# A recurrent scan's transfers on SyncE in a written order, weights fetched three tiles ahead, and a transposition queued late

## The chip, the cores and the metric

The kernel runs on one core of one Trainium2 chip. The metric is the device time of one execution in microseconds. The core has TensorE (PE in the profile; its weight loads are PEld), VectorE (DVE), ScalarE (ACT), GpSimd (POOL) and SyncE (SP). Each takes its instructions in order; DMAs are started here by SyncE or ScalarE, and the start stands in that engine's order (SPq, ACTq).

## The reference, cut to what matters

A two-layer decoder trunk over 272 tokens (16 learned ones and 256 given), model width 2048, all float32. The first layer mixes tokens with an RWKV-7 recurrence, the second with stick-breaking attention; each is followed by a SwiGLU block. The change touches the recurrence alone: for each of 32 heads of width 64

```python
def step(state, inp):
    r_t, d_t, k_t, v_t, kk_t, a_t = inp
    sa = jnp.einsum('bhvk,bhk->bhv', state, -kk_t)
    state = (state * d_t[:, :, None, :]
             + sa[..., None] * (kk_t * a_t)[:, :, None, :]
             + v_t[..., None] * k_t[:, :, None, :])
    return state, jnp.einsum('bhvk,bhk->bhv', state, r_t)
...
_, y = lax.scan(step, s0, tuple(seq_first(t) for t in (rh, dh, kh, vh, kk, ah)))
y = seq_first(y)
...
y = ((y - mean) * lax.rsqrt(var + GN_EPS)).reshape(b, l, d) * gn_w + gn_b
bonus = (jnp.sum(rh * kh * r_k, axis=-1, keepdims=True) * vh).reshape(b, l, d)
out = ((y + bonus).astype(h.dtype) * g) @ w_o
```

with `r`, `k`, `v` from the products of the shifted tokens with `w_r`, `w_k`, `w_v`, and the decay, the rate `a` and the gate `g` from small two-step (low-rank) products.

## The kernel before, in words

Tokens lie along the free axis (272 columns), features along the 128 partitions. A product of float32 weights is made in three matmuls: `split` (or the two lines L167 and L168 of `parts`) turns a weight tile `raw` into a rounded part `whi` (ScalarE) and the rest `wlo` (VectorE), and `mm3k` (L186 to L188) multiplies `whi` by both parts of the activations and `wlo` by the first.

The recurrence is worked in four chunks of 64 tokens and one of 16, for a pair of heads at a time: 16 pairs, class `Pair`. `scan` runs a software pipeline over periods n = -3 to 15. In period n four pairs are at work: C (pair n+3) makes its decay and rate in `lora`; B (n+2) makes its scores, has the 16x16 diagonal blocks of its triangular system solved on GpSimd in `solve`, and lays out its operands; M (n+1) joins the solved blocks into 64x64 inverses in `left(16)`, `right(16)`, `left(32)`, `right(32)`, then `apply` and `trans`; A (n) passes the state through the chunks in `states` and `step`, and then `norm` and `gate` make its output `o` (L1286). Between these calls `f` takes a few steps of `stream`, which multiplies the tokens by the big weights `w_v`, `w_r` and at the end `w_o`: 32 steps of three matmuls in a full period, so four tiles `raw` of 512 KB; `raw` has three buffers, `whi` and `wlo` six each.

The order of TensorE in the scan is that of the program, written out by hand (`manual_schedule`). All other engines, and SyncE's transfers with them, are ordered when the kernel is built by a planner, which places what it expects to be ready, by its own times.

The path of a pair's solve, with the lines in the profile: scores `G` (VectorE, L1071) go by DMA to a scratch tile `s1` in DRAM (L1076, L1078: four issues), the diagonal blocks come back as `As` (L1080); GpSimd solves them into `Ts` (L1109 to L1116); `Ts` goes by DMA to `s2` (L1118), and 64x64 tiles `Tt` come back (L1121, two issues). All eight are issued from ScalarE (`self.dq = nc.scalar`). `left` transposes `Tt` into `Tn` on VectorE (L1170) and multiplies `Tt` (`yb`, L1174); `right` multiplies with `Tn` (`zb`, L1193) and adds to `Tt` (L1194). `apply` ends with `Ah` (VectorE, L1209), which `trans` multiplies (`rm`, L1221). `norm` sums squares over each head on TensorE (`vb`, L951), takes a logarithm and an exponential on ScalarE (L1271, L1272, each with a load of its function table), and goes on with five VectorE instructions (L1273 to L1277); `gate` adds `o`.

The small weights of a pair (`w2` in `split_w`, L933: 128 KB each; the name in the trace is `lora`) and the norms `rn` (L961) come by SyncE, as the big weights do (L156).

## The time and the profile before

| | us |
|---|---|
| median of 3 runs | 2808.99 (2807.55 to 2813.99) |
| the profiled execution's own time | 2810.86 |
| its span, first to last instruction | 2809.0 |
| TensorE busy in the span | 2688.8 |
| VectorE, ScalarE, GpSimd busy | 1797.5, 1489.9, 178.8 |
| mean granted TensorE clock | 0.981 of full speed |

The profile is of one execution. "Busy" is the union of an engine's instructions. A line of the view of waits reads: who waited, for whom, how long in total, how often, the longest. A line of the timeline reads: start, duration, engine and line, operation, what it writes from what, how many, and in brackets the idle time of the engine before it with what ended it. The scan lies where GpSimd solves: its L1116 starts first at 209.4 and last at 708.1 us.

### The profile page before, as it was taken

Reading aid. Unit: us, or ns where it says so; the run is one execution under the profiler, and the core shown is the slowest. Engines: PE = TensorE matmul, PEld = TensorE weight load, DVE = VectorE, ACT = ScalarE, POOL = GpSimd, SP = SyncE. Lnnn points to the kernel's source line nnn. Section 1 sums busy time; section 2 is a strip of 40 time slices with the busy share of each in tenths; the row PEclk is TensorE's granted clock in tenths of the full one; section 3 lists DMA queues with packets and bytes.
Section 4 is the critical chain, followed back from the end, with each engine's and each line's share of the span. In section 5 each row is a group of like instructions: output and inputs, shape, how many; then the busy total and the mean of one; then the engine's idle time right before and its main releaser. Section 6 shows DMA issues by size and latency. Waiting matters only on the chain.

```text
span 2809.0 us, 54126 instructions
## 1 busy us (share of the span) xinstructions
PE 2688.8 (96%) x20942; PEld 2484.5 (88%) x20942; DVE 1797.5 (64%) x3586; ACT 1489.9 (53%) x3005; POOL 178.8 (6%) x539
## 2 busy tenths in 40 slices
PE   7987888888899999999999999999999999999999
PEld 5787777777799999999999999988888888888888
DVE  6665666666466555555555776577776666666666
ACT  6664555555455444444444665477655455455554
POOL 0004333333000000000000000000000000000000
PEclk9999999999899999999999999999999999999999
DMA  5443333332455555555565555533456565665655
GB/s 178 128 127 101 96 92 86 86 85 77 137 170 179 166 185 176 165 186 175 166 186 176 164 178 166 173 128 120 156 186 188 184 193 178 200 188 179 196 185 175
DMA packets 185330, 439.50 MB, mean 156 GB/s; under 512 B 58448, under 2 KB 88688, under 8 KB 185072
## 3 DMA queue, kind: packets, MB, share of 16 engines
q1 hardware_dynamic: 140240, 426.67, 48.0%
q10 hardware_dynamic: 44832, 9.38, 1.7%
q8 instruction: 164, 2.69, 0.4%
q14 instruction: 94, 0.77, 0.1%
HBM read 430.24 MB, written 5.74 MB: 155 GB/s over the span
## 4 chain that ended last, share of the span: by engine, by line
PE 83%; POOL 6%; DMA 4%; ACT 2%; DVE 2%; issue 2%; ACTq 1%; POOLq 0%; DVEq 0%; SPq 0%
PE mm L192 22%; PE mm L186 14%; PE mm L188 14%; PE mm L187 14%; PE mm L191 11%; POOL Ts L1116 3%; POOL Tm L1114 3%; PE lr L540 1%; DMA As<-s 1%; DMA s<-Ts 1%; DMA raw<-w_k 1%; ACT whi L167 1%; PE cb L1255 1%; DMA s<-G 1%; PE hms L791 1%
## 5 line engine op out<-in xcount | busy, mean ns | idle before, releaser
L168 DVE TENSOR_TENSOR wlo<-raw,whi 128x512 fp32r<-128x512 f32 (+1 forms) x1588 | 1076.6, 682 | 676.5 <-ACT whi L167 655.5
L167 ACT CAST whi<-raw 128x512 fp32r<-128x512 f32 (+1 forms) x1588 | 962.3, 611 | 946.0 <-PE mm L187 558.5
L186 PE MATMUL mm<-hl,whi 128*128 128x272 f32 x3344 | 982.2, 294 | 6.8 <-ACT whi L167 5.1
L188 PE MATMUL mm<-hl,wlo 128*128 128x272 f32 x3344 | 973.7, 291 | 4.0 <-DVE wlo L168 4.0
L187 PE MATMUL mm<-hl,whi 128*128 128x272 f32 x3344 | 971.0, 290 | 0.0
L192 PE MATMUL mm<-hl,whi 128*128 128x512 f32 x2624 | 920.0, 395 | 0.0
L191 PE MATMUL mm<-hl,wlo 128*128 128x256 f32 x2624 | 740.8, 283 | 0.0
L186 PEld LDWEIGHTS mm<-hl,whi 128*128 128x128 f32 x3344 | 636.6, 190 | 19.0 <-issue 8.6
L187 PEld LDWEIGHTS mm<-hl,whi 128*128 128x128 f32 x3344 | 643.1, 192 | 0.6
L188 PEld LDWEIGHTS mm<-hl,wlo 128*128 128x128 f32 x3344 | 637.0, 191 | 6.3 <-DVE wlo L168 4.7
L192 PEld LDWEIGHTS mm<-hl,whi 128*128 128x128 f32 x2624 | 492.5, 188 | 113.0
L191 PEld LDWEIGHTS mm<-hl,wlo 128*128 128x128 f32 x2624 | 494.2, 188 | 0.6
L208 DVE TENSOR_TENSOR h<-h,mm 128x256 f32<-128x256 f32 (+1 forms) x224 | 94.0, 421 | 6.6 <-PE mm L192 6.0
L186 PE MATMUL mm<-hi,whi 128*128 128x272 f32 x256 | 80.8, 316 | 0.0
L201 ACT COPY c<-mm 128x256 f32<-128x256 f32 x104 | 38.8, 373 | 78.8 <-PE mm L192 78.7
L1116 POOL TENSOR_TENSOR Ts<-Ts,Tm 40x14 f32<-40x14 f32 (+6 forms) x224 | 77.7, 347 | 17.5
L1114 POOL TENSOR_TENSOR Tm<-Ts,As 40x14 f32<-40x14 f32 (+6 forms) x224 | 75.5, 337 | 17.5
L187 PE MATMUL mm<-lo,whi 128*128 128x272 f32 x256 | 74.9, 293 | 0.0
L188 PE MATMUL mm<-hi,wlo 128*128 128x272 f32 x256 | 74.6, 291 | 0.0
L1221 PE MATMUL rm<-G,Ah 64*64 64x128 f32 x256 | 16.0, 383 | 43.8 <-DVE Ah L1209 43.8
L186 PEld LDWEIGHTS mm<-hi,whi 128*128 128x128 f32 x256 | 49.0, 192 | 5.6 <-issue 2.7
L1221 PEld LDWEIGHTS rm<-G,Ah 64*64 64x64 f32 x256 | 10.4, 186 | 47.1 <-DVE Ah L1209 46.4
(287 smaller groups left out, 2343.6 us busy)
## 6 DMA issues: line engine op xcount, KB each, us to landing
raw<-w_gate SPq DMA_DIRECT2D x176, 512.0 KB
raw<-w_up SPq DMA_DIRECT2D x176, 512.0 KB
raw<-w_down SPq DMA_DIRECT2D x128, 512.0 KB
raw<-w_down SPq DMA_DIRECT2D x128, 192.0 KB
raw<-w_v SPq DMA_DIRECT2D x32, 512.0 KB
raw<-w_r SPq DMA_DIRECT2D x32, 512.0 KB
raw<-sb_w_k SPq DMA_DIRECT2D x32, 512.0 KB
raw<-sb_w_v SPq DMA_DIRECT2D x32, 512.0 KB
```

Source lines behind the costliest of these rows:

```text
L167: nc.scalar.copy(hi, part)
L168: nc.vector.tensor_tensor(lo, part, hi.bitcast(F32), ALU.subtract)
L186: mm(out, w[0], x[0], start=first, stop=False)
L187: mm(out, w[0], x[1], start=False, stop=False)
L188: mm(out, w[1], x[0], start=False, stop=last)
L191: mm(out[:, :n], w[1], x[0], start=first, stop=False, skip_group_check=True)
L192: mm(out, w[0], x[2], start=False, stop=last, skip_group_check=True)
L201: self.nc.scalar.copy(c, out[:, n:])
L208: self.nc.vector.tensor_tensor(h, h, out[:, c:c + n], ALU.add)
L540: nc.tensor.matmul(bk[i, j][:c, :T], w[i, j][:, k % 4 * c:k % 4 * c + c], x, start=k == 0, stop=k == NK - 1)
L1114: V.tensor_tensor(t, Ts[:, 0:i, i:i + 1].to_broadcast([40, i, n]), As[:, i:i + 1, i + 1:].to_broadcast([40, i, n]), ALU.mult)
L1116: V.tensor_tensor(Ts[:, 0:i, i + 1:], Ts[:, 0:i, i + 1:], t, ALU.add)
```

## The change

- All transfers of the scan are issued from SyncE (`dq` is `nc.sync`), and SyncE's order in the scan is the program's, like TensorE's.
- `solve` is cut in two: GpSimd's part stays, and the transfers of `Ts` to `s2` and of `s2` to `Tt` move into `inverse`, which is called for M at the head of the next period.
- The big weights run through one generator, `chunks`: at its start three tiles are requested, each further one is requested when both halves of the tile three before it have been split, and halves are split one ahead of their use.
- The small weights are requested after `left(32)` of the period before: `load_gate` for M, `load_lora` for pair n+4.
- Each `Tn` (L1170) is queued on VectorE behind `b.last`, which is `o` of A's gate in that period (or, before there is an A, the last instruction of B's `bonus`).

```diff
-            self.dq = nc.scalar
+            self.dq = nc.sync
...
-            with tc.manual_schedule(engines={mybir.EngineType.PE}):
+            with tc.manual_schedule(engines={mybir.EngineType.PE, mybir.EngineType.SP}):
                 self.scan(sp)
...
+        pairs[0].load_lora()
         for n in range(-3, NK):
             get = lambda i: pairs.get(n + i)
             A, M, B, C = get(0), get(1), get(2), get(3)
             f = fill if C else lambda k: fill(k / 2)
+            if M:
+                M.inverse()
...
                 f(3 if g[0] == "trans" else 4)
+                if g == ("left", 32):
+                    if M:
+                        M.load_gate()
+                    if get(4):
+                        get(4).load_lora()
...
+    def chunks(self, jobs):
+        nc = self.nc
+        todo = [(src, j, min(j + 8, n)) for src, n in jobs for j in range(0, n, 8)]
+        raws = []
+
+        def load():
+            if len(raws) < len(todo):
+                src, j0, j1 = todo[len(raws)]
+                raw = self.wraw.tile([128, (j1 - j0) * 128], F32, name="raw", tag="raw")
+                nc.sync.dma_start(raw, src[:, j0 * 128:j1 * 128])
+                raws.append(raw)
...
+        for _ in range(NRAW):
+            load()
+        ahead = None
+        for i, (src, j0, j1) in enumerate(todo):
+            for k in range(0, j1 - j0, 4):
+                w = split(raws[i], k, min(k + 4, j1 - j0))
+                if k + 4 >= j1 - j0:
+                    load()
+                if ahead:
+                    yield from ahead
+                ahead = w
+        yield from ahead
...
+    def load_w(self, lo, hi):
+        raw = self.b.l2.tile([128, hi - lo], F32, name="w2", tag="w2", bufs=2)
+        self.nc.sync.dma_start(raw, self.b.a["lora2"][self.p][:, lo:hi])
+        return raw
+
+    def load_lora(self):
+        p = self.p
+        self.da = self.load_w(0, 256)
+        self.rn = self.t272("rn")
+        self.nc.sync.dma_start(
+            self.rn, self.b.rkd[2 * p:2 * p + 2].unsqueeze(1).to_broadcast([2, 64, T]))
+
+    def load_gate(self):
+        self.g = self.load_w(256, 512)
...
     def bonus(self):
...
-        self.V.tensor_tensor(self.bv, self.v, bp, ALU.mult)
+        self.b.last = self.V.tensor_tensor(self.bv, self.v, bp, ALU.mult)
...
+        self.Ts = Ts
+
+    def inverse(self):
+        b = self.b
         s2 = b.s2[self.p % 2]
-        b.dq.dma_start(self.diag(s2), Ts)
+        b.dq.dma_start(self.diag(s2), self.Ts)
         self.Tt = self.big("Tt", 5, 64)
...
-        V.transpose(self.Tn.rearrange(flat), Tt[:, :4].rearrange(flat))
+        with b.tc.issue_after(b.last.ins):
+            V.transpose(self.Tn.rearrange(flat), Tt[:, :4].rearrange(flat))
...
     def gate(self):
...
-        self.V.scalar_tensor_tensor(o, self.y, self.vec("gn_b"), gp[:, :T], ALU.add, ALU.mult)
+        b.last = self.V.scalar_tensor_tensor(o, self.y, self.vec("gn_b"), gp[:, :T], ALU.add, ALU.mult)
```

## The prediction

> **What bounds the kernel now.** I read first the page's chain (what ended last, by engine), then busy time in stretches (start and end in us, length, then each engine's busy time and count, TensorE's clock, DMA share, GB/s), then TensorE's waits inside the stretch that is not full.

> ```profile
> PE 83%; POOL 6%; DMA 4%; ACT 2%; DVE 2%; issue 2%; ACTq 1%; POOLq 0%; DVEq 0%; SPq 0%
> ```
> ```profile
> core 0: us, PE busy (x) PEld busy (x) DVE busy (x) ACT busy (x) POOL busy (x), PEclk, DMA share, GB/s
> 284.36:311.45 27.09, 26.66 (x362) 23.66 (x360) 17.52 (x45) 15.48 (x39) 10.98 (x33) 1.00 0.33 91
> 315.58:344.95 29.37, 28.86 (x360) 25.62 (x360) 18.05 (x47) 15.94 (x40) 10.91 (x33) 0.91 0.27 79
> 447.80:477.56 29.76, 29.17 (x360) 26.00 (x360) 18.27 (x47) 15.82 (x40) 10.47 (x33) 0.89 0.26 77
> 480.80:509.52 28.72, 27.96 (x360) 24.95 (x360) 18.14 (x46) 15.78 (x40) 10.97 (x33) 0.94 0.30 86
> ...
> 200.00:740.00 540.00, 461.80 (x5773) 409.35 (x5772) 319.71 (x792) 276.79 (x673) 176.72 (x522) 0.92 0.30 84
> 740.00:2809.00 2069.00, 2059.12 (x14157) 1932.62 (x14155) 1351.02 (x2493) 1084.12 (x2042) 0.00 (x0) 1.00 0.56 176
> ```
> ```profile
> PE rm L1221 <- DVE Ah L1209: 43.8, 11, 6.3
> ...
> PE wa L1204 <- DVE Tt L1194: 7.1, 2, 3.8
> ...
> PE cb L1247 <- ACT X L1211: 2.8, 1, 2.8
> PE mm L186 <- ACT whi L167: 2.7, 1, 2.7
> ...
> PE tv L1137 <- ACT An L1097: 1.8, 1, 1.8
> ```

> TensorE carries 83% of the chain. Behind 740 us it is busy in 2059 of 2069 us at clock 1.00, and the change does not reach there. In the scan (200 to 740) it is idle for 78 of 540 us and its clock is 0.92. The waits between 200 and 740, TensorE's alone, say where: `rm` on `Ah`, 11 times 4 us. I take all five rows as one cause, together 58.2 us. In one period the timeline of TensorE, ScalarE and VectorE shows the links:

> ```profile
> 441.02 1.09 PE L1204 MATMUL wa<-X,Tt 64*64 64x128 f32 x16
> ...
> 447.80 1.15 PE L1221 MATMUL rm<-G,Ah 64*64 64x128 f32 x16 [3.99 <-DVE Ah L1209]
> ```
> ```profile
> 442.29 0.28 ACTq L1118 DMA_DIRECT2D s<-Ts  x1
> 442.61 0.41 ACT L936 CAST dah<-w 128x256 fp32r<-128x256 f32 x1 [5.71 <-POOL Ts L1116]
> ...
> 444.69 1.28 ACTq L1121 DMA_DIRECT2D Tt<-s  x2
> 446.06 1.14 ACT L167 CAST whi<-raw 128x512 fp32r<-128x512 f32 x2 [1.51 <-issue]
> ```
> ```profile
> 446.71 0.69 DVE L168 TENSOR_TENSOR wlo<-raw,whi 128x512 fp32r<-128x512 f32 x1 [1.43 <-ACT whi L167]
> 447.32 0.42 DVE L1209 COPY Ah<-wa 128x256 f32<-128x256 f32 x1
> ```

> ScalarE stands 5.7 us at the issue of `Ts`, which waits for GpSimd, then 1.5 us around `Tt`'s issue. VectorE's `wlo` waits for ScalarE's cast, `Ah` stands behind `wlo`, and `rm` behind `Ah`, though `wa` had ended at 442.1. After such a stall the clock is halved for a while: from `rm` to the next stall the same work took 27.09 us in the stretch at clock 1.00 and 29.37, 29.76 and 28.72 (mean 29.3) in those at 0.89 to 0.94. So a stall costs its length and 2.2 us.

> **The change part by part.** *Issues leave ScalarE.* Their waits go with them, and with them the five waits: -58.2 us, and 2.2 us of half clock for each of 14 long stalls (11 + 2 + 1), -31 us. What comes late next at `rm` is nothing that I see: `Ah` (0.42 us) follows `wa` at once while twelve fill matmuls run.

> *SyncE takes them.* Eight more issues a period, at most 0.65 us each by the row of `Tt` (1.28 for two), are about 5 of 33 us. In its written order `Ts` waits for GpSimd, `Tt` for `Ts` to land, `As` for the scores; behind each stand big and small weights. These have three `raw` tiles and six halves, together six tiles, of which a period of 33 us (447.80 to 480.80 above) uses four: a hold of 15 us is two tiles, and covered; without that cover each us of it is one of TensorE. I cost it at nothing.

> *The result fetched at the next head.*

> ```profile
> 449.78 0.45 DVE L1170 STREAM_TRANSPOSE Tn<-Tt 128x256 f32<-128x256 f32 x1 [2.04 <-DMA Tt<-s]
> ```
> ```profile
> 451.21 0.40 PE L1240 MATMUL cb<-SC,WV 64*64 64x16 f32 x4
> ...
> 464.47 0.27 PE L1174 MATMUL yb<-Tt,An 64*64 64x64 f32 x2
> ```

> From issue (442.29) to use took 7.5 us. Issued as late as the next head (`cb<-SC`, 451.21), `Tt` is there at 458.7; `yb` reads it at 464.5. Cost nothing, with 5.8 us to spare.

> *The transposition behind `o`.* This is the part with a price. `zb` needs `Tn`, and `Tn` may now not pass A's `o`, whose chain starts at `vb` shortly before:

> ```profile
> 428.36 0.29 PE L952 MATMUL vb<-lo,blk 128*128 128x272 f32 x1
> ...
> 433.56 0.68 PE L1193 MATMUL zb<-Ys,Tn 64*64 64x64 f32 x16
> ```
> ```profile
> 429.51 1.28 ACT L1271 ACT_TABLE_LOAD   x1
> 430.80 0.49 ACT L1271 ACTIVATE rs<-vb,dv 128x272 f32<-128x272 f32 x1
> 431.97 0.37 ACT L1159 COPY X<-kv 64x256 f32<-64x256 f32 x1 [0.68 <-PE kv L1153]
> 432.36 1.28 ACT L1272 ACT_TABLE_LOAD   x1
> 433.65 0.43 ACT L1272 ACTIVATE rs<-rs 128x272 f32<-128x272 f32 x1
> ```
> ```profile
> 434.11 0.44 DVE L1273 TENSOR_TENSOR sq<-rs 128x272 f32<-128x272 f32 x1 [1.33 <-ACT rs L1272]
> ...
> 437.06 0.78 DVE L168 TENSOR_TENSOR wlo<-raw,whi 128x512 fp32r<-128x512 f32 x1
> 437.76 0.48 DVE L1286 SCALAR_TENSOR_TENSOR o<-y,vecs,gp 128x272 f32<-128x272 f32 x1
> ```
> ```profile
> 735.90 0.39 PE L952 MATMUL vb<-lo,blk 128*128 128x272 f32 x1
> ```
> ```profile
> 738.95 0.44 DVE L1273 TENSOR_TENSOR sq<-rs 128x272 f32<-128x272 f32 x1 [3.10 <-ACT rs L1272]
> ...
> 741.55 0.50 DVE L1286 SCALAR_TENSOR_TENSOR o<-y,vecs,gp 128x272 f32<-128x272 f32 x1
> ```

> TensorE goes from `vb` (ends 428.65) to `zb` (433.56) in 4.9 us, and its order does not change. The chain takes longer. With ScalarE's order as it is, the exponential ends at 434.08. The VectorE part from `sq` to `o` starts 2.6 us apart in the last pair, where nothing lies between (738.95, 741.55); before, `Tt`'s addition and `Tn` itself lay there and now cannot. So `o` starts at 436.7 and ends at 437.2, `Tn` adds 0.45, a hand-over 0.1: `zb` at 437.7, 4.1 us late. Lower end: the last pair's chain without company, 735.90+0.39=736.29 to 741.55+0.50=742.05, is 5.8 us, with `Tn` 6.3, so 1.4 us late. Upper end: two `wlo` of 0.7 us in the chain, 5.5. I take 3.9, near the row of the middle pair, a little less since ScalarE loses its issues. M and A are both there for n = 0 to 14: 14 full pairs, 54.6 us, and the last of them, which has hardly company, 1.4 us. With 14 long stalls the half clock comes back too: +31 us.

> [...] After a gap of 3.37 us the clock was 0.50:

> ```profile
> 546.45 0.51 PE L1221 MATMUL rm<-G,Ah 64*64 64x128 f32 x4 [3.37 <-DVE Ah L1209]
> ```
> ```profile
> 547.00:549.50 2.50, 2.50 (x20) 2.17 (x13) 0.55 (x2) 0.58 (x2) 0.00 (x0) 0.50 0.35 113
> ```

> [...]

> *The start.* The scan's first small weight, for which ScalarE waited before, is now ahead of the big ones in SyncE's order:

> ```profile
> 182.95 0.40 ACT L936 CAST dah<-w 128x256 fp32r<-128x256 f32 x1 [1.41 <-DMA w<-lora]
> ```

> Before, no wait for a big tile stands there. Now the first goes out behind `lora` and `rn` (0.65 us each at most, as above) and is split after `dah`: I take +1.5 us, between 0 and the 5 us of a TensorE that waits for a whole transfer.

> Sum: -58.2 -31 +54.6 +1.4 +31 +1.5 = -0.7 us on the profiled execution of 2810.9 (whose span is 2809.0); the median shown lies 1.9 below it. So 2808 for the median: a stall is moved from `rm` to `zb`.

> **The rivals.** A, faster: the planner lays the chain denser once it gates TensorE. For it: 0.86 us pass between `vb` and the first table load (428.65 to 429.51), 0.68 in a copy that waits for `kv`. Against: that order stood in the same place with the issues in it. At 3.0 us late it is 14 x 0.9 = 13 us less, 2796; at the 1.4 us end, where the clock also stays up, 35 + 31 us less, 2742.

> B, slower: casts and `wlo` of the fills slip between the five VectorE steps, as one did before `o` (437.06). Two make 5.3 us late: +20, 2828. From 4.3 us late on, by 0.4 x 14, it is slower.

> C, the change does not do what it says: `Ah` still waits for a `wlo` whose cast is late, half of the old stalls stay, +29 +15: 2852. Against: ScalarE's long waits all are the issues'.

> D, faster: the new stalls, amid dense matmuls, do not halve the clock: 31 us less, 2777. Against: the row of 3.37 us, shorter than 3.9. [...]

> **How the numbers follow.** 0.2% (5.6 us) is about what a measurement of this kernel can tell. Forecast 0.42, with `zb` 3.5 to 4.3 us late, of it 0.28 inside the 5.6 us, 0.08 faster, 0.06 slower; A 0.28; B 0.20; C 0.05; D 0.05. Faster 0.08+0.28+0.05 = 0.41, same 0.28, slower 0.06+0.20+0.05 = 0.31. The forecast's own range is 2801 to 2815. For 8 in 10 the range goes to 2768, half-way into A's lower end, and to 2832, past B, leaving C and the rest of A.

> **What would show it.** In the changed profile: no `dah` or `whi` of ScalarE waiting for GpSimd; the row `rm` on `Ah` gone; a new row, `zb` on `Tn`, of some 13 to 15 times 3.9 us; `Tn` following `o` within 0.5 us; the clock of 200 to 740 still near 0.92 and the scan still 540 us long. If that row is short, A or D; if it is over 4.3 us, B. A wait of TensorE for `whi` or `Tt` behind SyncE, or of GpSimd for `As` longer than now, would make the costs that I set to nothing wrong.

## The result and the profile after

The changed kernel takes 2814.61 us (median of 20 runs, 2812.25 to 2818.75), the kernel before 2810.91 us beside it (20 runs): ratio 1.0015, 95% interval 1.0008 to 1.0022. So it is slower by 3.7 us where -1 was forecast: inside the 5.6 us that were called no change, but on the other side of zero. The profiled execution took 2815.13 us, 4.3 more than that of before.

The chain by engine, of the changed kernel:

```profile
PE 88%; DVE 4%; ACT 3%; DMA 3%; issue 2%; POOL 0%; SPq 0%; ACTq 0%; DVEq 0%
```

GpSimd's 6% have left the chain, and VectorE has twice its share. TensorE's waits between 190 and 745 us (total, times, longest):

```profile
PE zb L1250 <- DVE Tn L1227: 60.7, 14, 4.6
PE zb L1250 <- ACT hl L249: 4.5, 1, 4.5
...
PE cb L1312 <- ACT S L1314: 2.9, 7, 0.5
...
PE yb L1231 <- DMA Tt<-s: 0.3, 1, 0.3
```

All five rows that the prediction added up are gone. In their place stands `zb`, 15 times, together 65.2 us. Busy time in stretches (columns as in the prediction), first of before, then of after, from the first `zw` to the last `o`:

```profile
183.40:286.40 103.00, 88.72 (x950) 81.44 (x950) 60.71 (x148) 48.06 (x123) 38.10 (x103) 0.91 0.36 106
286.40:684.20 397.80, 341.98 (x4323) 303.17 (x4322) 246.44 (x612) 211.36 (x516) 129.65 (x394) 0.93 0.31 86
684.20:742.00 57.80, 48.48 (x631) 41.64 (x630) 25.47 (x63) 26.19 (x56) 9.83 (x29) 0.89 0.18 52
```
```profile
190.40:285.80 95.40, 86.20 (x951) 78.94 (x950) 61.03 (x150) 49.13 (x122) 36.23 (x103) 0.94 0.41 122
285.80:688.00 402.20, 344.14 (x4321) 308.54 (x4320) 248.99 (x613) 213.92 (x516) 131.73 (x394) 0.91 0.33 87
688.00:747.70 59.70, 48.97 (x631) 42.09 (x630) 25.20 (x64) 26.31 (x56) 9.60 (x29) 0.91 0.19 54
```

The three stretches are the filling of the pipeline, twelve full periods and its end. From one to the other kernel: the scan starts 7.0 us later (183.4 to 190.4), fills 7.6 us faster, takes 4.4 us more for the full periods and 1.9 more at its end; behind it 1.4 us are won: +4.3. TensorE is busy for 479.2 us in the first three rows and for 479.3 in the second three, so the half clock costs the same in both; its idle time is 79.4 before and 78.0 after.

A full period of the changed kernel, in the middle. TensorE, then ScalarE, then VectorE:

```profile
429.04 0.29 PE L1005 MATMUL vb<-lo,blk 128*128 128x272 f32 x1
...
438.86 1.12 PE L1250 MATMUL zb<-Ys,Tn 64*64 64x64 f32 x16 [4.54 <-DVE Tn L1227]
```
```profile
428.49 1.28 ACT L1328 ACT_TABLE_LOAD   x1
429.79 0.49 ACT L1328 ACTIVATE rs<-vb,dv 128x272 f32<-128x272 f32 x1
430.29 1.28 ACT L1030 ACT_TABLE_LOAD   x1
...
432.34 0.41 ACT L1329 ACTIVATE rs<-rs 128x272 f32<-128x272 f32 x1
```
```profile
433.73 0.44 DVE L1330 TENSOR_TENSOR sq<-rs 128x272 f32<-128x272 f32 x1
...
434.22 0.41 DVE L1068 TENSOR_TENSOR BK<-kk,Q 128x256 f32<-128x256 f32 x1
...
434.91 0.41 DVE L1236 TENSOR_TENSOR Ys<-yb,consts 128x256 f32<-128x256 f32 x1
...
436.07 0.75 DVE L704 TENSOR_TENSOR wlo<-raw,whi 128x512 fp32r<-128x512 f32 x1
436.75 0.51 DVE L1334 SCALAR_TENSOR_TENSOR y<-y,dv,bv 128x272 f32<-128x272 f32 x1
437.18 0.76 DVE L704 TENSOR_TENSOR wlo<-raw,whi 128x512 fp32r<-128x512 f32 x1
437.87 0.48 DVE L1343 SCALAR_TENSOR_TENSOR o<-y,vecs,gp 128x272 f32<-128x272 f32 x1
438.28 0.43 DVE L1227 STREAM_TRANSPOSE Tn<-Tt 128x256 f32<-128x256 f32 x1
```

`Tn` follows `o` at once and `zb` follows `Tn`: the queue is what TensorE waits for. ScalarE's part of the chain is shorter than forecast (its exponential ends 3.4 us after `vb`, 432.75 against 429.33; before it was 5.4), since the first table load is already under way when `vb` ends. VectorE's part is longer: 4.1 us from `sq` to `o`, not 2.6, with two `wlo`, `BK`, `Ys` and smaller ones between the five steps.

The start, SyncE, ScalarE and TensorE:

```profile
179.29 0.33 SPq L971 DMA_DIRECT2D w<-lora  x1
...
180.37 0.90 SPq L695 DMA_DIRECT2D raw<-w_v  x2
```
```profile
187.95 2.42 ACT L703 CAST whi<-raw 128x512 fp32r<-128x512 f32 x4 [3.85 <-DMA raw<-w_v]
```
```profile
188.62 0.60 PE L186 MATMUL mm<-hl,whi 128*128 128x272 f32 x1 [9.49 <-ACT whi L703]
```

TensorE's first matmuls of the scan are fills with big weights, ahead of `zw` in its order, and the first big tile, requested at 180.4, is there at 187.9: `zw` runs at 190.4. In the kernel before, SyncE requested the first of these two tiles 23.3 us earlier, while the stage ahead of the scan still ran:

```profile
157.07 4.84 SPq L156 DMA_DIRECT2D raw<-w_v  x2
```

In the changed kernel its written order holds the tiles behind `lora`, which goes out at 179.3.

### The profile page after: what moved, and what is told of

The parts are those of the page before. It is cut to its first block, busy times and chain, and to the rows that moved or that the text cites. A ratio compares the mean times of both kernels' runs of the same rounds, so it can differ in the third digit from the quotient of the medians.

```text
span 2813.3 us, 54147 instructions
## 1 busy us (share of the span) xinstructions
PE 2688.5 (96%) x20942; PEld 2487.2 (88%) x20942; DVE 1798.6 (64%) x3586; ACT 1492.6 (53%) x3005; POOL 178.8 (6%) x539
## 4 chain that ended last, share of the span: by engine, by line
PE 88%; DVE 4%; ACT 3%; DMA 3%; issue 2%; POOL 0%; SPq 0%; ACTq 0%; DVEq 0%
PE mm L192 22%; PE mm L186 16%; PE mm L188 15%; PE mm L187 15%; PE mm L191 11%; PE lr L540 1%; PE zb L1250 1%; DMA raw<-w_k 1%; DMA raw<-w_r 1%; PE cb L1312 1%; PE hms L831 1%; ACT L1030 1%; PE wa L1261 1%; PE yb L1231 1%; PE cb L1304 1%
## 5 line engine op out<-in xcount | busy, mean ns | idle before, releaser
L168 DVE TENSOR_TENSOR wlo<-raw,whi 128x512 fp32r<-128x512 f32 (+1 forms) x1448 | 979.0, 679 | 621.1 <-ACT whi L167 601.4
L167 ACT CAST whi<-raw 128x512 fp32r<-128x512 f32 (+1 forms) x1448 | 879.3, 610 | 877.0 <-PE mm L187 542.2
L186 PE MATMUL mm<-hl,whi 128*128 128x272 f32 x3344 | 976.1, 292 | 13.4 <-ACT whi L703 9.5
L186 PEld LDWEIGHTS mm<-hl,whi 128*128 128x128 f32 x3344 | 631.5, 189 | 23.9 <-ACT whi L703 10.0
L704 DVE TENSOR_TENSOR wlo<-raw,whi 128x512 fp32r<-128x512 f32 x140 | 99.1, 715 | 80.6 <-ACT whi L703 79.7
L703 ACT CAST whi<-raw 128x512 fp32r<-128x512 f32 x140 | 86.0, 620 | 62.7 <-PE mm L187 40.1
L1250 PE MATMUL zb<-Ys,Tn 64*64 64x64 f32 x512 | 27.8, 263 | 65.2 <-DVE Tn L1227 60.7
L186 PE MATMUL mm<-hi,whi 128*128 128x272 f32 x256 | 88.9, 347 | 0.0
L1250 PEld LDWEIGHTS zb<-Ys,Tn 64*64 64x64 f32 x512 | 23.1, 170 | 70.8 <-issue 64.0
L187 PE MATMUL mm<-lo,whi 128*128 128x272 f32 x256 | 81.7, 319 | 0.0
```

The costliest lines, as they stand in the source:

```text
L167: nc.scalar.copy(hi, part)
L168: nc.vector.tensor_tensor(lo, part, hi.bitcast(F32), ALU.subtract)
L186: mm(out, w[0], x[0], start=first, stop=False)
L187: mm(out, w[0], x[1], start=False, stop=False)
L703: nc.scalar.copy(hi, part)
L704: nc.vector.tensor_tensor(lo, part, hi.bitcast(F32), ALU.subtract)
```

## The experiments

My theory: the queue behind `o` (the rule `issue_after`, by which `Tn` comes behind `o` in VectorE's order) gives back what the issues' move to SyncE gains, and the late first tile adds 7 us. The rivals: the issues themselves gain little; or the stall at `zb` costs less than it shows, since other waits and the clock take its place. All ratios are to the kernel before on the same chip. A difference to the changed kernel is one of medians from different rounds; the kernel before took 2808.4 to 2809.8 us beside the experiments and 2810.9 beside the changed kernel, so up to 2.5 us of such a difference are not the edit's. Line numbers shift a little from kernel to kernel.

**The queue taken away, in two ways.** Once the planner places `Tn`, and once `Tn` stays queued, but behind B's `bonus` instead of A's `o`.

```diff
-        with b.tc.issue_after(b.last.ins):
-            V.transpose(self.Tn.rearrange(flat), Tt[:, :4].rearrange(flat))
+        V.transpose(self.Tn.rearrange(flat), Tt[:, :4].rearrange(flat))
```

> The changed kernel with Tn's place on VectorE left to the planner again. Theory 1 (the stall at zb is there only because Tn stands behind o; each costs 4.55 us and about 2.2 us of half clock): the row 'zb on Tn' (60.7 us in 14) falls to under 10 us and the time to about 2720 us (2814.6 - 14 x 6.75), up to 2780 if VectorE now waits for Tt's landing in some periods. Theory 2 (something else, the solve's result or a full ScalarE or VectorE, sets the period, and zb is only where it shows): the wait turns up at another instruction and the time stays within 10 us of 2814.

```diff
     def gate(self):
-        b.last = self.V.scalar_tensor_tensor(o, self.y, self.vec("gn_b"), gp[:, :T], ALU.add, ALU.mult)
+        self.V.scalar_tensor_tensor(o, self.y, self.vec("gn_b"), gp[:, :T], ALU.add, ALU.mult)
```

> The changed kernel with every Tn queued behind the last instruction of B's bonus instead of behind A's o, which is some 13 us earlier in the period. Theory 1: zb no longer waits, about 14 x (4.55 + 2.2) = 94 us less, 2720 us, TensorE's clock of the scan from 0.92 to over 0.97. Theory 2: same time as the changed kernel within 10 us, with the wait at another place.

Measured: 2766.01 us without a queue, ratio 0.9849 (0.9827 to 0.9872), and 2740.44 us behind the bonus, 0.9750 (0.9736 to 0.9765). TensorE's longest waits in the scan, behind the bonus:

```profile
PE zb L1250 <- DVE Ys L1236: 15.9, 13, 1.7
```

and without a queue the longest, with VectorE's own wait for `Tt`:

```profile
PE bonus L1004 <- DVE G L1123: 20.8, 13, 3.4
```
```profile
DVE Tn L1226 <- DMA Tt<-s: 45.6, 15, 6.3
```

The wait on `Tn` is gone in both, and behind the bonus 74 us with it (2814.6 to 2740.4). From the first `zw` to the last `o` TensorE's idle time falls from 78.0 to 32.8 us and its busy time, in which the half clock shows, from 479.3 to 449.3. The first is the stall (65) less, in the main, 16 us of a shorter wait that comes late next: `Ys`, which VectorE makes among the same steps. The second, 30 us, is the half clock, for which the prediction had 31. The planner's own place is worse by 26 us: it sets `Tn` so early that VectorE stands up to 6.3 us until `Tt` has landed, with `G` behind it. TensorE's clock behind the bonus, the last figure but two:

```profile
200.00:660.00 460.00, 428.97 (x5728) 382.50 (x5726) 319.77 (x792) 275.49 (x670) 190.18 (x524) 0.99 0.37 103
```

0.99 where it was 0.92.

**Each part alone, in the kernel before.** First the queue without the issues' move, then the move without anything else.

```diff
-        self.V.tensor_tensor(self.bv, self.v, bp, ALU.mult)
+        self.b.last = self.V.tensor_tensor(self.bv, self.v, bp, ALU.mult)
...
-        V.transpose(self.Tn.rearrange(flat), Tt[:, :4].rearrange(flat))
+        with b.tc.issue_after(b.last.ins):
+            V.transpose(self.Tn.rearrange(flat), Tt[:, :4].rearrange(flat))
...
-        self.V.scalar_tensor_tensor(o, self.y, self.vec("gn_b"), gp[:, :T], ALU.add, ALU.mult)
+        b.last = self.V.scalar_tensor_tensor(o, self.y, self.vec("gn_b"), gp[:, :T], ALU.add, ALU.mult)
```

> The kernel before with nothing but the queueing of Tn behind o (transfers still from ScalarE, the planner's order for SyncE). Theory 1a (the two stalls overlap: zb's 4.5 us let GpSimd's solve and ScalarE's held casts go on meanwhile, so that rm finds Ah ready): 2805 to 2825 us, with 'zb on Tn' near 60 us and 'rm on Ah' under 10 us; then the move to SyncE gains nothing as long as Tn stands behind o. Theory 1b (the stalls add up): 2811 + 14 x 6.75, about 2900 us, both rows there.

Measured: 2857.94 us, ratio 1.0172 (1.0154 to 1.0190).

```profile
PE zb L1194 <- DVE Tn L1171: 77.3, 14, 11.3
PE yb L1175 <- DVE Tt L1195: 10.9, 11, 1.9
```

There is no row of `rm` on `Ah`. The queue alone takes that stall away, puts a longer one at `zb`, adds small ones behind it, and costs 48 us. This lies between a stall that only moves and two that add up.

```diff
-            self.dq = nc.scalar
+            self.dq = nc.sync
```

> The kernel before with one line changed: the scan's transfers are issued from SyncE, in the planner's order, nothing else. Theory 1 (the stalls at rm come from ScalarE standing at the issues of Ts and Tt): 'ScalarE waiting for GpSimd' (59 us before) is gone, 'rm on Ah' (43.8 us) falls under 10 us, and the time to 2740 to 2780 us. Rival (without a written order, SyncE holds big weights behind Ts as ScalarE held casts): the scan waits for whi in place of Ah, 2795 us or more.

Measured: 2823.34 us, ratio 1.0050 (1.0035 to 1.0065). A row of TensorE's waits, one of VectorE's, and VectorE's timeline:

```profile
PE rm L1221 <- DVE Ah L1209: 61.0, 13, 6.0
```
```profile
DVE Tn L1170 <- DMA Tt<-s: 93.5, 15, 7.6
```
```profile
455.86 0.45 DVE L1170 STREAM_TRANSPOSE Tn<-Tt 128x256 f32<-128x256 f32 x1 [6.86 <-DMA Tt<-s]
456.23 0.38 DVE L1209 COPY Ah<-wa 128x256 f32<-128x256 f32 x1
```

The stall at `rm` stays, and grows, with no issue on ScalarE. No cast of `whi` makes `Ah` late here: with the issues gone the planner lays VectorE's order anew and puts `Tn`, whose `Tt` is still on its way, right ahead of `Ah` in 13 of 16 periods (before, in the middle period, `Ah` came first, at 447.32, and `Tn` at 449.78). So the move to SyncE does not free `Ah` by itself; the place of `Tn` has to change with it. The queue does that, and it also takes the stall at `rm` away with the issues still on ScalarE, as the run before this one shows. Without a queue `rm` has no row in the first experiment either; that this comes from the fetch a period later is likely and not shown, since SyncE's written order and the tiles three ahead are in that run too, and none of the three was run alone. Neither of the theories written down named this.

**The first tiles ahead.** The three first big tiles requested ahead of `lora` and `rn`, nothing else changed.

```diff
     def scan(self, sp):
+        a = self.a
+        self.wgen = self.chunks([(a[n][p], NK) for p in range(NK) for n in ("w_v", "w_r")]
+                                + [(a["w_o"][m][:, :KHEAD * 128], KHEAD) for m in range(NHEAD)])
+        next(self.wgen)
...
         pairs[0].load_lora()
...
         for _ in range(NRAW):
             load()
+        yield None
```

> The changed kernel with the first three weight tiles requested ahead of the first small weight, so the scan's start is as in the kernel before. Theory 1 (7 us are lost at the start, since the first weight tile now goes out behind lora and rn at 180 us): TensorE's first product of the scan comes some 5 to 7 us earlier and the time is about 2808 us. Rival: the start is made good in the first periods anyway: 2814 us.

Measured: 2807.12 us, ratio 0.9992 (0.9982 to 1.0001), that is 7.5 us less than the changed kernel. The first `zw` of this run, on TensorE:

```profile
180.65 0.59 PE L186 MATMUL zw<-dec_w1h,dah 96*128 96x272 f32 x1 [4.28 <-ACT dah L993]
```

It now waits for its own small weight only; the first tile was requested at 155.4. The stalls at `zb` are as long as in the changed kernel (61.0 and 4.6). The late start did not buy the faster filling: the first `o` comes 80.1 us behind the first `zw` here (260.8) and 80.3 in the changed kernel (270.8). So the start accounts for its 7 us (7.5 by the medians, 6.4 with each kernel set against its own kernel before), and without it the change is what was forecast, none.

**The queue behind an earlier step.** `Tn` behind the third of the five steps of the norm (`rs<-sq`, L1332), so that a short stall is left.

```diff
-        V.scalar_tensor_tensor(rs2, sq, -3.0, rs2, ALU.add, ALU.mult)
+        self.b.last = V.scalar_tensor_tensor(rs2, sq, -3.0, rs2, ALU.add, ALU.mult)
...
-        b.last = self.V.scalar_tensor_tensor(o, self.y, self.vec("gn_b"), gp[:, :T], ALU.add, ALU.mult)
+        self.V.scalar_tensor_tensor(o, self.y, self.vec("gn_b"), gp[:, :T], ALU.add, ALU.mult)
```

> The changed kernel with Tn queued behind the third of the five VectorE steps of A's norm (rs<-sq) instead of behind o: a smaller dose of the same delay. In the changed kernel that step starts 2.6 us before o. Theory 1: the row 'zb on Tn' falls from 4.55 to about 1.9 us a period, so 14 x 2.65 = 37 us less; and if a stall of 1.9 us leaves the clock up, some 26 us more: 2750 us; if it still halves it, 2777 us. Theory 2 (zb's wait does not depend on where Tn stands): 2814 us.

Measured: 2758.15 us, ratio 0.9819 (0.9804 to 0.9834); the waits, one of them on TensorE's timeline, and two stretches:

```profile
PE zb L1250 <- DVE Tn L1227: 24.2, 13, 2.0
PE zb L1250 <- DVE Ys L1236: 4.8, 2, 2.7
```
```profile
296.46 0.68 PE L1250 MATMUL zb<-Ys,Tn 64*64 64x64 f32 x16 [1.98 <-DVE Tn L1227]
```
```profile
200.00:690.00 490.00, 449.70 (x5820) 401.44 (x5818) 322.03 (x803) 281.09 (x680) 186.61 (x524) 0.96 0.36 97
...
297.10:300.51 3.41, 3.41 (x22) 3.16 (x22) 2.62 (x6) 0.62 (x1) 2.86 (x8) 0.50 0.20 24
```

The stall shrinks to 1.9 us, and the time by 56. From the first `zw` to the last `o` TensorE's idle time falls by 37.5 us (78.0 to 40.5), of which the waits at `zb` are 36 (65.2 to 29.0), and its busy time by 18.5 (479.3 to 460.8), which is the clock: over 200 to 690 us it went from 0.92 to 0.96. Behind 8 of the 13 stalls it was still halved, for 3.41 us each, as in the last row; behind the other five it was not.

**The rests of the fills behind `o`.** To see whether the two `wlo` are what makes `o` late, all `wlo` of the big weights are queued behind `o` and the `Tn` that follows it; this `Tn` is asked for right behind A's gate (`flip`).

```diff
                 A.gate()
+                if M:
+                    M.flip()
...
+        return self.tc.issue_after(last.ins) if last else contextlib.nullcontext()
...
-            nc.vector.tensor_tensor(lo, part, hi.bitcast(F32), ALU.subtract)
+            with self.behind():
+                nc.vector.tensor_tensor(lo, part, hi.bitcast(F32), ALU.subtract)
...
+        with b.tc.issue_after(b.last.ins):
+            b.last = V.transpose(self.Tn.rearrange(flat), Tt[:, :4].rearrange(flat))
```

> The changed kernel with the rests wlo of the big weights queued behind A's o and the transposition behind it, so that none can lie between the VectorE steps of the norm. Theory (rival B in part): the 4.55 us at zb are longer than the forecast's 3.9 because two wlo of 0.75 us lie ahead of o; without them zb waits 4.55 - 1.5 = 3.1 us, 14 x 1.5 = 21 us less, 2794 us, with the half clock unchanged. If the later rests make matmuls wait in turn, a row mm on wlo shows it. Rival: the two wlo only fill holes in which VectorE waits anyway (for ScalarE or for B's operands); zb's wait stays over 4.2 us and the time over 2808.

Measured: 2803.94 us, ratio 0.9985 (0.9977 to 0.9994), 10.7 us less than the changed kernel by the medians (8.2 with each set against its own kernel before). TensorE's waits in the scan, then `vb` and VectorE's order in the middle of it:

```profile
PE mm L188 <- DVE wlo L712: 56.0, 14, 4.8
PE zb L1271 <- DVE Tn L1236: 7.0, 2, 3.8
```
```profile
423.58 0.29 PE L1013 MATMUL vb<-lo,blk 128*128 128x272 f32 x1
```
```profile
431.68 0.44 DVE L1236 STREAM_TRANSPOSE Tn<-Tt 128x256 f32<-128x256 f32 x1
432.04 2.04 DVE L712 TENSOR_TENSOR wlo<-raw,whi 128x512 fp32r<-128x512 f32 x3
```

`Tn` ends at 432.12, 8.25 us after `vb` (423.87); in the changed kernel 9.4 (438.71 less 429.33). The two `wlo` cost 1.1 us of the chain, not 1.5: part of their time lay in holes. The wait itself did not go; it moved from `zb` to the fill ahead of it, which needs a `wlo` from behind `Tn`. The expectation had named this row as a possible sign; the time lies between the two that it gave.

**Both repairs, and a later logarithm.** The first tiles ahead and `Tn` behind the bonus together; and with them the logarithm of the norm behind the exponential `Q` of C's `lora` on ScalarE, to take the wait on `Ys` away.

> The changed kernel with Tn queued behind B's bonus and the first weight tiles requested ahead of the first small weight, together. If the two causes are apart, their effects add: 2740 - 7.5 = 2733 us. If the start is made good by the now shorter periods: 2740.

```diff
-        A.activation(Q, L, AF.Exp, scale=-1.0)
+        b.lastq = A.activation(Q, L, AF.Exp, scale=-1.0)
...
-        A.activation(rs2, vb, AF.Ln, bias=self.b.gneps)
+        with self.b.tc.issue_after(self.b.lastq.ins):
+            A.activation(rs2, vb, AF.Ln, bias=self.b.gneps)
```

> The same two changes, and A's logarithm queued on ScalarE behind the last exponential of C's lora, as it stood in the kernel before. In the run with Tn behind bonus, zb still waited 13 times 1.2 us for Ys, behind lora's VectorE work, which had waited 1.3 us for those exponentials. Theory: that wait goes, 13 us less than the kernel without it, about 2720 us. Rival: the norm chain, now later, makes another wait of the same size: 2733 us.

Measured: 2735.16 us, ratio 0.9744 (0.9727 to 0.9761), and 2732.62 us, ratio 0.9732 (0.9718 to 0.9747); the two intervals overlap. The longest wait of the first, then of the second:

```profile
PE zb L1254 <- DVE Ys L1240: 14.5, 12, 1.7
```
```profile
PE yb L1235 <- DVE Tt L1255: 14.6, 13, 1.3
```

The two repairs nearly add up (74 and 7.5 from 2814.6 make 2733); the interval of the ratio, 2732 to 2741 us, does not rule out 2740, at which the start would add nothing. Where the wait on `Ys` is taken away, one as long stands a step later, at `yb`. The change with `Tn` behind the bonus and the first tiles ahead is 2.6% faster than the kernel before.

## Why the prediction held in the main and missed the sign

*The mechanism held.* A stall of TensorE moves from `rm` to `zb`, the clock of 200 to 740 us stays (0.92 before, 0.91 after), and the sum of TensorE's idle time and half clock hardly changes (79.4 to 78.0 us idle, 479.2 to 479.3 busy). Taking the stall away gave 74 us, so it is what eats the gain.

*The term that failed is the start.* +1.5 us was put down, 7.0 measured, and 7.5 won back when the first tiles went ahead. The step said that the first tile goes out behind `lora` and `rn` and priced their two issues. What it left out: the kernel before had requested that tile at 157.1, and in the written order it goes out at 180.4 only. TensorE's order has fills ahead of `zw`, so `zw` waits for the whole transfer of a tile (180.4 to 187.9), which was given as the upper end, 5 us, and is longer still. These 5.5 us are more than the 5.0 between forecast and profiled time (-0.7 and +4.3).

*`zb`.* 14 stalls of 3.9 us and one of 1.4, 56.0 us, were forecast; 65.2 were measured, 4.5 us in a full period. From `vb`'s end to `zb` the middle period needs 9.5 us where 9.05 came out of the working. ScalarE's part is 2.0 us shorter than forecast; `sq` then starts 1.0 us behind the exponential, after B's operands; and the 2.6 us from `sq` to `o`, taken from the last pair where nothing lies between, are 4.1. That the holes are filled is rival B's mechanism, though by the experiment the two `wlo` account for 1.1 us only; B's point, 4.3 us, was passed by a little. The last pair's stall was taken too short as well (2.8 us for 1.4). An omission of the other sign balances this, by luck: three small rows that I had left out went too, `cb` on `S`, `zb` on `Ys` and `yb` on `Tt`. Before:

```profile
PE cb L1255 <- ACT S L1257: 7.2, 15, 1.7
...
PE zb L1193 <- DVE Ys L1179: 3.1, 6, 1.9
...
PE yb L1174 <- DVE Tt L1194: 2.2, 3, 1.1
```

They make 12.5 us, of which 2.9 and 0.3 are left: -9.3, against the +9.2 of `zb`.

*The issues.* "Issues leave ScalarE, and with them the five waits" is right for the whole change and wrong as a step of its own: moved alone they leave the stall at `rm` in place (61.0 us) and cost 0.5%. The working followed the chain of the old order and kept that order; the planner made another. Rival C foresaw that `Ah` might stay late, by another mechanism; in the whole change it did not come.

*At nothing:* SyncE's holds and the late fetch of `Tt` did cost nothing. TensorE waits for `Tt` once, 0.3 us. ScalarE has a new long wait, `gh` for its late weight (61.2 us in 13 waits, 5.5 at most), which no row of TensorE's waits names.

*The clock.* It was forecast that stalls of 3.9 us halve it as that of 3.37 had, and those of 4.5 us did (about the middle one it was 0.50 from 437.6 to 444.3 us); rival D is wrong. The stalls of 1.9 us show that length alone does not decide: 8 of 13 halved it, for 3.41 us each, and the last section shows which.

## What to carry to other kernels

Where a planner orders an engine, a wait that is taken away changes that order: look up what will then stand ahead of the late instruction, before the whole wait is counted as gained. An instruction that waits for a DMA should be queued behind a step that ends about when the data lands, neither ahead of that nor behind the last step there is: here the place of one transposition of 0.43 us decided between 2740 and 2815 us. And where first requests change places, follow the first matmul in the written order to the tile that it needs.

## What was not expected of the hardware

In the run with those stalls each of the eight stalls lay whole in one slot: the one before 296.46 fills 294.48 to 296.46 of the slot that ends at 297.11. The five that were spared were cut by the end of a slot. One of them, from 354.67 to 356.54, in its two slots and the next:

```profile
351.72:355.13 3.41, 2.95 (x54) 2.51 (x53) 2.72 (x9) 3.36 (x11) 2.61 (x7) 1.00 0.64 249
355.13:358.55 3.42, 2.02 (x27) 1.98 (x28) 3.42 (x11) 1.15 (x5) 2.77 (x9) 1.00 0.00 0
358.55:361.96 3.41, 3.41 (x52) 2.98 (x51) 3.41 (x6) 1.46 (x3) 2.94 (x7) 1.00 0.50 129
```

TensorE is idle for 0.46 us of the first slot and 1.40 of the second, and the clock stays up. Between 200 and 745 us of the traces of before and after, 30 slots at full clock held over 1.85 us of idle time, and a slot at half clock followed every one; of 225 with less than 1.04 us, none. Of the 11 between, 3 were followed by half the clock, so idle time by these records is not all that counts, and what else does stays open. Behind the bonus, where the thirteen waits on `Ys` are 1.7 us at most, the clock over 200 to 660 us was 0.99.
